# A hybrid attention, state-space and ConvFFN block on one core: other order of products and shared sums in Down's last group, an own bank for its right columns, and two up pairs with the value half first

## The chip, the cores and the metric

One Trainium2 chip, of which the kernel uses one core. The metric is the device time of one execution in microseconds (us), taken as the median over several runs; the profile is of one further execution. Engines go by short names: PE is TensorE (matmuls into PSUM banks), DVE is VectorE, ACT is ScalarE, POOL is GpSimd, SP is SyncE, which here only starts transfers. A queue (SPq, ACTq) is an engine's own list of transfers to start.

## The reference

One layer: a normed input goes through attention and a state-space model side by side, the merged result through an output projection, then a gated feed-forward part with a causal convolution of width 3, and a last norm. All in float32; 1024 tokens after 16 meta tokens, model width 1024, feed-forward width 2816. The change lies in the last two lines of this cut:

```
def _rmsnorm(x, g):
    xf = x.astype(jnp.float32)
    y = xf * lax.rsqrt(jnp.mean(xf * xf, axis=-1, keepdims=True) + RMS_EPS)
    return (y * g.astype(jnp.float32)).astype(x.dtype)

def _conv_ffn(xn, w_up, conv_w, conv_b, w_down):
    seq_len = xn.shape[1]
    hid = xn @ w_up
    hp = jnp.pad(hid, ((0, 0), (CONV_WIDTH - 1, 0), (0, 0)))
    conv = conv_b + sum(hp[:, j:j + seq_len] * conv_w[j] for j in range(CONV_WIDTH))
    val, gate = jnp.split(conv, 2, axis=-1)
    return (jax.nn.silu(gate) * val) @ w_down
...
        xn = _rmsnorm(h, norm_ffn_g[layer])
        h = h + _conv_ffn(xn, w_ffn_up[layer], ffn_conv_w[layer], ffn_conv_b[layer],
                          w_ffn_down[layer])
    h = _rmsnorm(h, norm_final_g)
    return h[:, N_META:]
```

## The kernel before

**A float32 product as three matmuls.** Every operand is cut into a high part (a cast on ACT to the type fp32r) and a low part (source minus high part, `split_lo`, line 137, on DVE or POOL). A product is then high·high + high·low + low·high. The pair of cuts of one operand is called a form here.

**The up stage.** The feed-forward width is 22 blocks of 128 channels; block c of the value and block c of the gate are a pair. Pairs 0, 1, 2 and 21 are "plain" (`plain_steps`, line 1209): for each half the 1024 tokens are taken in parts of 342, 342 and 340, each part 8 × 3 matmuls into one PSUM bank; ACT then writes the first term of the convolution with its bias (line 1228), DVE adds the other two (line 1230). The gate's output is the tile `og`, of which one buffer exists, the value's is `ov`, of which two exist. When both are there, `glue` takes the silu of `og` on ACT, multiplies it into `ov` on POOL (line 1183), and starts the store to `a_d`. The plain pairs do the gate half first. While pairs 0 to 2 run, DVE also makes token forms (`xn_forms`, lines 1349 and 272 to 279) for the pairs 3 to 20, which are made in another way.

**The Down stage** (from line 1386) multiplies the 1024 × 2816 result by the down weights and adds it to the residual, held in eight tiles `hs0` to `hs7` (128 tokens × 1024). It halves all three dimensions, so that a 2 × 2 product of blocks takes seven products of half size instead of eight. `j` counts 11 slices of the inner dimension, in four groups, (8,9), (7,0,1), (2,3,4), (5,6,10). Each group runs the products p in the order 0, 4, 1, 2, 5, 3, 6 (`ORDER`); a product is four tiles t of 128 tokens, each 3 matmuls for every j of its group, so 9 in the last group, 512 columns wide. Upper tiles are `hs0` to `hs3`, lower ones `hs4` to `hs7`, and l_ and r_ their left and right 512 columns.

- *Banks.* Products 0, 1, 2 and 3 take four fresh banks, from one of two sets (`SETS`: banks named mm, mm, mm, po, or sp, tp, sp, tp). Products 4, 5 and 6 go on in the banks of 0, 1 and 3 (`JOINS`), on top of what is there, after DVE has read it.
- *Results.* After each tile DVE adds the bank to where product p goes (line 1517): `u2[t]` (u20 to u23) for 0 and 2, the right half of the lower tile for 1 and 3, the left half of the upper for 4, of the lower for 5, and the right half of the upper for 6.
- *Shared sums.* What `u2` holds after product 2 goes into three places, on POOL (line 1528): the lower tile's left and right half and the upper tile's right half. In groups before the last, `u2` goes on to the next group and is not yet used, so that these sums exist in the last group only: 12 of 128 × 512.
- *Norm.* When a half tile is final, ACT squares it and sums the squares (`square`, line 1476), DVE adds that to the other half's (`va`, line 1478), POOL takes the power −1/2 (`rs`, line 1483), and `finish` scales: the left half, already multiplied by the weight `gfB` on POOL (lines 1531 and 1534), on ACT (line 1486), the right half times `rs` and `gfB` on DVE (line 1484). A transfer of each half follows, from SP for the right one and from ACT for the left one.
- *Forms.* `prepare` makes the forms of coming products as far ahead as there are slots (`ops`), in the order of the products. The low parts are cut on POOL for products 0, 4 and 5, on DVE for the others.
- *The last product* (6) of the last group takes tile 3 in two parts, 288 and 224 columns, both in tile 3's bank.

**What sets the order.** The program gives the instructions and which data each needs. The build orders each engine's instructions by its own planner of time, so that order is not that of the text; `after(x, y)` puts x behind y. On the chip each engine runs its list in that order, and an instruction that has to wait holds up those behind it.

## Time and profile before

| | us |
|---|---|
| runs of the kernel | 1450.41, 1450.68, 1454.93 |
| median | 1450.68 |
| the profiled execution's own time | 1446.98 |
| its span in the profile | 1445.2 |
| granted TensorE clock, mean over the span | 0.997 of full speed |
| PE busy | 1422.3 |
| DVE, POOL, ACT busy | 1074.9, 760.8, 721.4 |

The span runs from the first to the last thing that the profiler recorded; the execution's own time is 1.78 us longer. Busy shares are means over a whole program of unlike stages. In the rows of a timeline stand the start in us from the span's begin, the length, the engine, the line, the instruction with its tiles (buffer numbers left out, so `hs` is any of eight), the shape, and in brackets how long the engine was idle before it and what ended that. Up pairs 0 to 2 lie at about 765 to 843 us, the last group of Down at about 1376 to 1437 us.

The same stretch by engine, from the view of windows (length, then busy us and count of PE, PE's weight load, DVE, ACT and POOL, the granted clock, the DMA engines' share and GB/s):

```
1384.00:1392.00 8.00, 8.00 (x37) 6.64 (x36) 7.83 (x6) 1.86 (x4) 7.10 (x5) 1.00 0.39 118
1392.00:1408.00 16.00, 16.00 (x73) 13.24 (x72) 14.73 (x23) 7.04 (x16) 7.12 (x6) 1.00 0.00 0
1408.00:1417.00 9.00, 9.00 (x41) 7.33 (x40) 4.21 (x7) 2.17 (x6) 9.00 (x8) 1.00 0.01 2
```

### The profile page before, as it was taken

The page shows a single profiled execution, that of the slowest core. Times are in us where ns is not written, and L with a number is a line of the kernel's source. Part 1 is how long each engine was busy: PE and PEld are TensorE (multiplying, and loading weights), DVE is VectorE, ACT ScalarE, POOL GpSimd, SP SyncE. Part 2 cuts the span into 40 slices and gives each one's busy share as a digit, 9 for nine tenths or more (in the row PEclk, how much of TensorE's full clock was granted, in tenths as well). Part 3 has the DMA queues.
Part 4 walks back from the last instruction along what each step waited for, and adds up shares of the span by engine and source line. Part 5 has one row for each costly group of instructions (what it writes and reads, how often), then busy time and mean ns, then how long its engine had stood idle before and what let it go on. Part 6 is the DMA issues. An engine that isn't in the chain of part 4 may idle for free.

```text
span 1445.2 us, 26585 instructions
## 1 busy us (share of the span) xinstructions
PE 1422.3 (98%) x9646; PEld 1346.2 (93%) x9646; DVE 1074.9 (74%) x2199; ACT 721.4 (50%) x1421; POOL 760.8 (53%) x887
## 2 busy tenths in 40 slices
PE   8999999999999999999999999999999999999996
PEld 8999999988999999999889999999999999888885
DVE  7999798833667675656479977788876776789695
ACT  7647585423646565533646444434444445644333
POOL 1542248632456556425861335555555544887866
PEclk9999999999999999999999999999999999999998
DMA  8675644520147412177954246667743327964343
GB/s 302 172 179 164 163 102 146 166 83 31 47 141 166 114 59 78 31 245 251 247 149 145 76 110 168 178 160 189 190 138 111 97 80 255 328 204 146 104 93 117
DMA packets 92968, 214.06 MB, mean 148 GB/s; under 512 B 15090, under 2 KB 22898, under 8 KB 92452
## 3 DMA queue, kind: packets, MB, share of 16 engines
q1 hardware_dynamic: 73124, 166.32, 34.6%
q0 software_dynamic: 17696, 41.29, 14.9%
q10 hardware_dynamic: 2016, 4.74, 0.9%
q8 instruction: 76, 1.25, 0.4%
q14 instruction: 56, 0.46, 0.1%
HBM read 170.88 MB, written 71.71 MB: 168 GB/s over the span
## 4 chain that ended last, share of the span: by engine, by line
PE 93%; DVE 4%; issue 1%; ACT 1%; DMA 1%; POOL 0%; DVEq 0%; SPq 0%; ACTq 0%
PE mm L172 5%; PE mm L170 5%; PE mm L171 5%; PE sp L232 4%; PE sp L233 4%; PE sp L234 4%; PE tp L232 3%; PE tp L233 3%; PE tp L234 3%; PE mm L234 3%; PE mm L232 3%; PE mm L233 3%; PE tp L860 3%; PE mm L1509 2%; PE mm L1507 2%; PE mm L1508 2%
## 5 line engine op out<-in xcount | busy, mean ns | idle before, releaser
L170 PE MATMUL mm<-xhi,whi 128*128 128x342 f32 (+2 forms) x480 | 156.8, 327 | 1.0 <-DVE q L137 1.0
L172 PE MATMUL mm<-xhi,wlo 128*128 128x342 f32 (+2 forms) x480 | 155.3, 324 | 0.0
L171 PE MATMUL mm<-xlo,whi 128*128 128x342 f32 (+2 forms) x480 | 155.2, 324 | 0.0
L1183 POOL TENSOR_TENSOR ov<-ov,og 128x1024 f32<-128x1024 f32 x21 | 51.0, 2428 | 116.5 <-ACT og L1182 112.6
L137 DVE TENSOR_TENSOR sw<-sf,sw 128x512 fp32r<-128x512 f32 x72 | 72.5, 1007 | 45.9 <-ACT sw L1174 45.9
L1174 ACT CAST sw<-sf 128x512 fp32r<-128x512 f32 x72 | 44.9, 624 | 112.3 <-POOL sf L1318 87.5
L170 PEld LDWEIGHTS mm<-xhi,whi 128*128 128x128 f32 x480 | 90.5, 188 | 2.1 <-PE sp L818 0.8
L172 PEld LDWEIGHTS mm<-xhi,wlo 128*128 128x128 f32 x480 | 90.3, 188 | 0.5 <-issue 0.2
L171 PEld LDWEIGHTS mm<-xlo,whi 128*128 128x128 f32 x480 | 90.4, 188 | 0.2
L867 ACT CAST th<-tp 128x256 fp32r<-128x256 f32 (+3 forms) x120 | 56.1, 471 | 62.1 <-PE tp L860 29.8
L1318 POOL TENSOR_TENSOR sf<-raw,sf 128x512 f32<-128x512 f32 x36 | 63.7, 1769 | 40.0 <-DVE sw L137 39.9
L137 DVE TENSOR_TENSOR tl<-tp,th 128x256 fp32r<-128x256 f32 (+3 forms) x120 | 65.2, 547 | 26.0 <-ACT th L867 24.6
L1318 POOL TENSOR_TENSOR sf<-raw 128x512 f32<-128x512 f32 x36 | 48.2, 1338 | 65.0 <-DMA raw<-in_w_up_dram 39.8
L234 PE MATMUL mm<-xhi,sw 128*128 128x258 f32 (+1 forms) x288 | 81.0, 281 | 0.0
L232 PE MATMUL mm<-xhi,sw 128*128 128x258 f32 (+1 forms) x288 | 80.8, 281 | 0.0
L233 PE MATMUL mm<-xlo,sw 128*128 128x258 f32 (+1 forms) x288 | 80.7, 280 | 0.0
L832 POOL TENSOR_SCALAR pt<-pt,nm 128x144 f32<-128x144 f32 (+4 forms) x72 | 52.2, 738 | 50.9 <-DVE nm L831 49.9
L1370 DVE SCALAR_TENSOR_TENSOR ov<-hv,cwt,ov 128x1024 f32<-128x1024 f32 x36 | 69.5, 1930 | 0.4 <-ACT ov L1368 0.4
L1174 ACT CAST sw<-raw 128x512 fp32r<-128x512 f32 x70 | 43.0, 621 | 46.8 <-PE sp L234 22.8
L830 ACT ACTIVATE pt<-pt,nm 128x144 f32<-128x144 f32 (+4 forms) x72 | 52.9, 735 | 25.9 <-DVE nm L829 25.5
L823 DVE CUSTOM_DVE_ANT_0 pt<-sp,fb 128x328 f32<-128x328 f32 (+8 forms) x112 | 46.5, 430 | 20.6 <-PE sp L818 12.1
L137 DVE TENSOR_TENSOR sw<-raw,sw 128x512 fp32r<-128x512 f32 x70 | 57.8, 828 | 4.4 <-ACT sw L1174 4.4
(716 smaller groups left out, 5708.3 us busy)
## 6 DMA issues: line engine op xcount, KB each, us to landing
raw<-in_w_up_dram SPq DMA_DIRECT2D x44, 512.0 KB, 3.7
t_d<-in_w_dn_dram POOLq DMA_DIRECT2D x44, 256.0 KB, 6.9
wr<-t_d SPq DMA_DIRECT2D x44, 256.0 KB, 3.4
ar<-a_d SPq DMA_DIRECT2D x41, 256.0 KB, 5.3
a_d<-ov SPq DMA_DIRECT2D x18, 512.0 KB, 2.6
wr<-in_w_dn_dram SPq DMA_DIRECT2D x33, 256.0 KB, 3.7
t_d<-in_w_dn_dram SPq DMA_DIRECT2D x22, 256.0 KB, 4.3
t_d<-t_d SPq DMA_DIRECT2D x22, 256.0 KB, 4.5
```

The source lines that it names most:

```text
L137: return eng.tensor_tensor(out_, src, hi.bitcast(F), ALU.subtract)
L170: yield PE.matmul(ps, whi[:, i, :], ahi[:, i], start=(i == 0), stop=False)
L171: yield PE.matmul(ps, whi[:, i, :], alo[:, i], start=False, stop=False)
L172: yield PE.matmul(ps, wlo[:, i, :], ahi[:, i], start=False, stop=(i == k - 1))
L232: PE.matmul(ps, a[0][:, i], bh, start=(i == 0 and not joins), stop=False, skip_group_check=True)
L233: PE.matmul(ps, a[0][:, i], bl, start=False, stop=False, skip_group_check=True)
L234: PE.matmul(ps, a[1][:, i], bh, start=False, stop=(i == kh - 1), skip_group_check=True)
L830: S.activation(pt[:n, :kc], pt[:n, :kc], AF.Exp, bias=nm[:n, 1:2], scale=0.125, accum_out=nm[:n, 2:3])
L867: S.copy(th[:kn, z:tw], tp[:kn, z:tw])
L1174: S.copy(hi, src)
L1318: sums.append(GP.tensor_tensor(f_, a, b, op))
L1370: V.scalar_tensor_tensor(out=o, in0=h_[:, j:SEQ + j], scalar=cwc(j, m), in1=o, op0=ALU.mult, op1=ALU.add)
```

## The change

**Plain pairs.** Pairs 1 and 2 do the value half first, then the gate half. Pairs 0 and 21 stay.

**Down, last group only:**

- The products run as 0, 2, 4, 1, 5, 3, 6, and their forms are prepared as 0, 1, 2, 4, 5, 3, 6. Product 2 now takes the other set of banks (mm, mm, mm, po).
- The shared sums are spread: after the tiles of product 2 the one into the lower tile's left half, after those of product 1 the one into its right half, after those of product 5 the one into the upper tile's right half. Their number is the same.
- Products 3 and 6 both take tile 3 in parts of 288 and 224 columns, in this order, as the last tile. The 224 columns of both have a bank of their own (`held["end"]`).
- The scale of a finished tile is put behind the next tile's add (`scale_last`). Tile 2's right half is scaled at the very end; for tile 3, the square of the last 224 columns is taken on DVE, and the right half is multiplied by `gfB` first and by `rs` then (`finish_end`).

**All groups:** the slots of the forms are a list in which a freed slot goes to the back, instead of a counter.

The diff, cut to what is spoken of:

```diff
@@ -1207,14 +1207,17 @@
         return ha.tile([P, SEQ], F, tag=tag, name=tag, bufs=OUTS[tag])
 
     def plain_steps(c, parts=(QBLK,), ws={}):
-        res = []
+        res = {}
         ws = dict(ws)
-        for part, (m, tag) in ((part, mt) for part in parts for mt in ((NFF + c, "og"), (c, "ov"))):
+        halves = ((NFF + c, "og"), (c, "ov"))
+        if c in (1, 2):
+            halves = halves[::-1]
+        for part, (m, tag) in ((part, mt) for part in parts for mt in halves):
...
             if part is parts[0]:
-                res.append(conv_out(m, tag))
-            w2, o = ws[m], res[int(m == c)]
+                res[tag] = conv_out(m, tag)
+            w2, o = ws[m], res[tag]
...
-        glue(*res, c)
+        glue(res["og"], res["ov"], c)
 
     def plain_pair(c):
         run(plain_steps(c))
...
-        slot = ops[n_op[0] % len(ops)]
-        n_op[0] += 1
+        slot = ops.pop(0)
...
-        held[p] = [b() for b in SETS[(g + (p == 1)) % 2]]
+        held[p] = [b() for b in SETS[(g + (p == 1 or p == 2 and g == len(groups) - 1)) % 2]]
         return held[p]
 
     ss = {}
 
-    def square(c, cols):
+    def square(c, cols, by_dve=False):
         s_ = dn.tile([P, 1], F, tag="ss", name="ss", bufs=4)
-        S.activation(sq[:, :cols.stop - cols.start], hs[c][:, cols], AF.Square, accum_out=s_)
+        if by_dve:
+            x_ = hs[c][:, cols]
+            last_ = V.tensor_tensor_reduce(out=u2[0][:, :cols.stop - cols.start], in0=x_, in1=x_, scale=1.0, scalar=0.0,
+                                           op0=ALU.mult, op1=ALU.add, accum_out=s_)
+        else:
+            last_ = S.activation(sq[:, :cols.stop - cols.start], hs[c][:, cols], AF.Square, accum_out=s_)
         va = dn.tile([P, 1], F, tag="va", name="va", bufs=12)
-        V.scalar_tensor_tensor(out=va, in0=s_, scalar=1.0 / D, in1=ss[c] if c in ss else eps, op0=ALU.mult, op1=ALU.add)
+        va_ = V.scalar_tensor_tensor(out=va, in0=s_, scalar=1.0 / D, in1=ss[c] if c in ss else eps, op0=ALU.mult, op1=ALU.add)
         ss[c] = va
-
-    def finish(c, a, b):
+        return last_, va_
+
+    behind_ = []
+
+    def scale_last(inst):
+
+        while behind_:
+            finish(behind_.pop(), inst)
+
+    def finish_end(c, times):
         rs = dn.tile([P, 1], F, tag="rs", name="rs", bufs=2)
         GP.tensor_tensor(rs, ss[c], nhalf, ALU.pow)
-        V.scalar_tensor_tensor(out=hs[c][:, b], in0=hs[c][:, b], scalar=rs, in1=gfB[:, b], op0=ALU.mult, op1=ALU.mult)
+        a_, b_ = HALF
+        sc_ = V.tensor_scalar(hs[c][:, b_], u2[c][:, a_], rs, None, ALU.mult)
+        after(sc_, times)
+        S.activation(hs[c][:, a_], hs[c][:, a_], AF.Copy, scale=rs)
+        SY.dma_start(out[P * c:P * c + P, b_], hs[c][:, b_])
+        S.dma_start(out[P * c:P * c + P, a_], hs[c][:, a_])
+
+    rs_of = []
+
+    def right_half(c, rs, inst):
+        b = slice(512, D)
+        st_ = V.scalar_tensor_tensor(out=hs[c][:, b], in0=hs[c][:, b], scalar=rs, in1=gfB[:, b], op0=ALU.mult,
+                                     op1=ALU.mult)
+        after(st_, inst)
         SY.dma_start(out[P * c:P * c + P, b], hs[c][:, b])
+        return st_
+
+    def finish(c, inst):
+        a = slice(0, 512)
+        rs = dn.tile([P, 1], F, tag="rs", name="rs", bufs=2)
+        GP.tensor_tensor(rs, ss[c], nhalf, ALU.pow)
+        if c == 2:
+            rs_of.append(rs)
+        else:
+            right_half(c, rs, inst)
         S.activation(hs[c][:, a], hs[c][:, a], AF.Copy, scale=rs)
         S.dma_start(out[P * c:P * c + P, a], hs[c][:, a])
 
@@ -1491,12 +1528,13 @@
         joins = p in JOINS
         whole = (0, 512)
         parts = [(t, whole) for t in range(4)]
-        if last and p == 6:
-
-            parts = [(0, whole), (1, whole), (3, (0, 288)), (2, whole), (3, (288, 224))]
+        if last and p in (3, 6):
+            parts[3:] = [(3, (0, 288)), (3, (288, 224))]
+            if p == 3:
+                held["end"] = m_ps()
         bks = banks(g, p)
         for t, (c0, n) in parts:
-            bk = bks[t]
+            bk = held["end"] if last and p in (3, 6) and c0 else bks[t]
             top, bot = hs[t], hs[4 + t]
             to_, o = {0: (u2[t], 0), 1: (bot, 512), 2: (u2[t], 0), 3: (bot, 512),
                       4: (top, 0), 5: (bot, 0), 6: (top, 512)}[p]
@@ -1517,16 +1555,25 @@
                 first_add.append(V.tensor_tensor(to, to, ps, ALU.subtract if p in MINUS else ALU.add))
             if g == 2 and p == 3:
                 GP.dma_start(bot, h_d[P * (4 + t):P * (4 + t) + P], accum_op=ALU.add)
+            if last and p in (3, 6):
+                scale_last(first_add[-1])
             if last and p == 6:
-                square(t, slice(512 + c0, 512 + c0 + n))
-                if (t, c0) == (3, 0):
-                    continue
+                sq_, va_ = square(t, slice(512 + c0, 512 + c0 + n), by_dve=c0 > 0)
+                if t == 3 and c0:
+                    times = V.tensor_tensor(u2[t], hs[t][:, 512:], gfB[:, r_], ALU.mult)
+                    after(times, va_)
+                    finish_end(3, right_half(2, rs_of.pop(), times))
+                if t < 3:
+                    behind_.append(t)
+                continue
+            if last and n == 288:
+                continue
             if not last:
                 continue
-            if p == 2:
-                for d_, op in ((bot[:, l_], ALU.add), (bot[:, r_], ALU.subtract), (top[:, r_], ALU.subtract)):
-                    GP.tensor_tensor(d_, d_, u2[t], op)
-            elif p == 4:
+            if p in (2, 1, 5):
+                d_, op = {2: (bot[:, l_], ALU.add), 1: (bot[:, r_], ALU.subtract), 5: (top[:, r_], ALU.subtract)}[p]
+                GP.tensor_tensor(d_, d_, u2[t], op)
+            if p == 4:
                 square(t, l_)
                 GP.tensor_tensor(top[:, l_], top[:, l_], gfB[:, l_], ALU.mult)
             elif p == 5:
@@ -1534,20 +1581,18 @@
                 GP.tensor_tensor(bot[:, l_], bot[:, l_], gfB[:, l_], ALU.mult)
             elif p == 3:
                 square(4 + t, r_)
-                finish(4 + t, l_, r_)
-            elif p == 6:
-                finish(t, l_, r_)
+                behind_.append(4 + t)
 
     ORDER = (0, 4, 1, 2, 5, 3, 6)
     items = [(g, p) for g in range(len(groups)) for p in ORDER]
+    turns = items[:-len(ORDER)] + [(len(groups) - 1, p) for p in (0, 2, 4, 1, 5, 3, 6)]
+    items[-len(ORDER):] = [(len(groups) - 1, p) for p in (0, 1, 2, 4, 5, 3, 6)]
     ready = {}
-    room = [len(ops)]
 
     def prepare():
 
-        while len(ready) < (len(items) if first_add else 3) and room[0] >= len(groups[items[len(ready)][0]]):
+        while len(ready) < (len(items) if first_add else 3) and len(ops) >= len(groups[items[len(ready)][0]]):
             g, p = items[len(ready)]
-            room[0] -= len(groups[g])
             if p == 0:
                 for j in groups[g]:
                     if j not in SUMMED:
@@ -1556,7 +1601,6 @@
 
...
-    for g, p in items:
+    for g, p in turns:
         prepare()
...
         product(g, p, ready[g, p], g == 0, g == len(groups) - 1)
-        room[0] += len(groups[g])
+        ops += ready[g, p]
```

**Where the instructions move.** Three places. Names: `u20` to `u23` are u2, `ar` and `wr` the raw operands, `op1` to `op5`, `xhi` and `xlo` the slots that hold forms, `ss` a sum of squares.

DVE in the last group, up to the add of product 1's tile 0 into hs4 (the row L1517 or L1555 with hs4). Before:

```order
L137 TENSOR_TENSOR op3_15183<-ar_16350,op3_15183 128x512
L137 TENSOR_TENSOR op3_15183<-wr_16698,op3_15183 128x512
L1517 TENSOR_TENSOR hs3_15230<-hs3_15230,tp_16565 128x512
L1478 SCALAR_TENSOR_TENSOR va_16666<-ss_16664,eps_15225 128x1
L137 TENSOR_TENSOR xhi_97<-ar_16332,xhi_97 128x512
L137 TENSOR_TENSOR xhi_97<-wr_16749,xhi_97 128x512
L137 TENSOR_TENSOR xhi_97<-ar_16340,xhi_97 128x512
L1517 TENSOR_TENSOR hs4_15235<-hs4_15235,mm_16705 128x512
```

Now:

```order
L137 TENSOR_TENSOR xlo_98<-wr_16760,xlo_98 128x512
L1555 TENSOR_TENSOR hs0_15227<-hs0_15227,sp_16562 128x512
L1555 TENSOR_TENSOR hs1_15228<-hs1_15228,tp_16563 128x512
L1484 SCALAR_TENSOR_TENSOR va_16705<-ss_16703,eps_15225 128x1
L1484 SCALAR_TENSOR_TENSOR va_16720<-ss_16718,eps_15225 128x1
L1555 TENSOR_TENSOR hs2_15229<-hs2_15229,sp_16564 128x512
L137 TENSOR_TENSOR xlo_98<-ar_16348,xlo_98 128x512
L137 TENSOR_TENSOR xlo_98<-wr_16767,xlo_98 128x512
L1555 TENSOR_TENSOR hs3_15230<-hs3_15230,tp_16565 128x512
L1484 SCALAR_TENSOR_TENSOR va_16735<-ss_16733,eps_15225 128x1
L1484 SCALAR_TENSOR_TENSOR va_16750<-ss_16748,eps_15225 128x1
L1555 TENSOR_TENSOR hs4_15235<-hs4_15235,mm_16774 128x512
```

Between product 0's last add (u23 from tp) and this add lie 9 form cuts, 4 adds from PSUM and 3 va before; now 12 form cuts (those of products 3 and 6 all), 8 adds (of products 2 and 4) and 4 va.

POOL, the first shared sums. Before, behind the four products of hs0 to hs3 with gfB:

```order
L1531 TENSOR_TENSOR hs2_15229<-hs2_15229,gfB_15222 128x512
L1531 TENSOR_TENSOR hs3_15230<-hs3_15230,gfB_15222 128x512
L1528 TENSOR_TENSOR hs4_15235<-hs4_15235,u20_15231 128x512 x2
L1528 TENSOR_TENSOR hs0_15227<-hs0_15227,u20_15231 128x512
L1528 TENSOR_TENSOR hs5_15236<-hs5_15236,u21_15232 128x512 x2
L1528 TENSOR_TENSOR hs1_15228<-hs1_15228,u21_15232 128x512
```

Now, right behind POOL's last own form cuts:

```order
L137 TENSOR_TENSOR op0_15180<-ar_16354,op0_15180 128x512
L137 TENSOR_TENSOR op0_15180<-wr_16618,op0_15180 128x512
L1575 TENSOR_TENSOR hs4_15235<-hs4_15235,u20_15231 128x512
L1575 TENSOR_TENSOR hs0_15227<-hs0_15227,u20_15231 128x512
L1575 TENSOR_TENSOR hs5_15236<-hs5_15236,u21_15232 128x512
L1575 TENSOR_TENSOR hs1_15228<-hs1_15228,u21_15232 128x512
```

Eight sums (hs4 to hs7 and hs0 to hs3) now stand ahead of the products with gfB, and four (hs4 to hs7) behind them; before, all twelve stood behind.

DVE at the end of the program. Before:

```order
L1517 TENSOR_TENSOR hs3_15230<-hs3_15230,tp_16889 128x288
L1484 SCALAR_TENSOR_TENSOR hs1_15228<-hs1_15228,rs_17004,gfB_15222 128x512
L1478 SCALAR_TENSOR_TENSOR va_17022<-ss_17020,va_16681 128x1
L1517 TENSOR_TENSOR hs3_15230<-hs3_15230,tp_16889 128x224
L1478 SCALAR_TENSOR_TENSOR va_17036<-ss_17034,va_16666 128x1
L1478 SCALAR_TENSOR_TENSOR va_17056<-ss_17054,va_17022 128x1
L1484 SCALAR_TENSOR_TENSOR hs2_15229<-hs2_15229,rs_17038,gfB_15222 128x512
L1484 SCALAR_TENSOR_TENSOR hs3_15230<-hs3_15230,rs_17058,gfB_15222 128x512
```

Now (the two ISA rows are the square with its sum):

```order
L1555 TENSOR_TENSOR hs3_15230<-hs3_15230,tp_16890 128x288
L1484 SCALAR_TENSOR_TENSOR va_17033<-ss_17031,va_16735 128x1
L1555 TENSOR_TENSOR hs3_15230<-hs3_15230,mm_16886 128x224
L1484 SCALAR_TENSOR_TENSOR va_17051<-ss_17049,va_16750 128x1
L1479 ISA u20_15231,ss_17063<-hs3_15230 128x224
L1479 ISA ss_17063 128x1
L1484 SCALAR_TENSOR_TENSOR va_17065<-ss_17063,va_17051 128x1
L1563 TENSOR_TENSOR u23_15234<-hs3_15230,gfB_15222 128x512
L1509 SCALAR_TENSOR_TENSOR hs2_15229<-hs2_15229,rs_17045,gfB_15222 128x512
L1499 TENSOR_SCALAR hs3_15230<-u23_15234,rs_17070 128x512
```

The 224 columns now come from a bank of their own (mm instead of tp), and the two last scales are preceded by the square and the product with gfB.

3 lines of the change are left out of this document (removed).

## The prediction, before the changed kernel was run

> **What bounds the kernel now.** I read the page first, then PE's waits, then the timeline of each engine around the two edited places. From the page, its head, PE's row and the chain of waits:
>
> ```profile
> span 1445.2 us, 26585 instructions
> PE 1422.3 (98%) x9646; PEld 1346.2 (93%) x9646; DVE 1074.9 (74%) x2199; ACT 721.4 (50%) x1421; POOL 760.8 (53%) x887
> PE 93%; DVE 4%; issue 1%; ACT 1%; DMA 1%; POOL 0%; DVEq 0%; SPq 0%; ACTq 0%
> ```
>
> PE is busy 98% of the span and the change takes no matmul away. So only gaps in PE, and what follows its last matmul, can move. The list of what PE waited for (total, times, longest) names the gaps:
>
> ```profile
> PE mm L351 <- ACT uh L409: 5.2, 1, 5.2
> PE tp L1507 <- DVE hs L1517: 3.6, 1, 3.6
> PE mm L1224 <- DVE og L1230: 1.6, 1, 1.6
> ```
>
> The first is at the start of the kernel and is not touched. The other two, 5.2 us together, are what the two edits can remove.
>
> **Part 1: pairs 1 and 2, value half first.** The timelines of PE, POOL, ACT and DVE (start, length, instruction, in brackets the idle time before it):
>
> ```profile
> 810.08 0.39 PE L1224 MATMUL mm<-xhi,sw 128*128 128x344 f32 x1 [1.65 <-DVE og L1230]
> 799.98 2.64 POOL L1183 TENSOR_TENSOR ov<-ov,og 128x1024 f32<-128x1024 f32 x1 [2.39 <-DVE ov L1230]
> 802.83 1.16 ACT L1228 ACTIVATE og<-mm,cwt 128x342 f32<-128x342 f32 x2
> 806.72 0.56 DVE L1230 SCALAR_TENSOR_TENSOR og<-mm,cwt,og 128x342 f32<-128x342 f32 x1
> 808.89 1.04 DVE L1230 SCALAR_TENSOR_TENSOR og<-mm,cwt,og 128x340 f32<-128x340 f32 x2
> ```
>
> The buffer og exists once. Pair 0's glue on POOL reads it until 802.62, so ACT cannot begin to empty pair 1's first gate bank before 802.83, though PE had filled it earlier. DVE's part follows at 806–810, and PE needs that bank again at 808.43. With the value half first the evictions go to ov, which has two buffers, and wait for no glue. They can start some 3 us earlier. Gate's evictions come one half later, when the glue is long over. I take the whole wait, −1.65. Bounds: that, since no other gap of PE lies there, and 0 if the same wait returns at a later bank (a rival below). The cover is the second ov buffer alone; without it the 1.65 is back.
>
> **Part 2: own bank for the right columns.** PE's and DVE's timelines at the end of the last product:
>
> ```profile
> 1429.68 0.39 PE L1507 MATMUL sp<-xhi 128*128 128x512 f32 x1
> 1431.04 0.29 PE L1507 MATMUL tp<-xhi 128*128 128x288 f32 x1
> 1432.09 0.29 PE L1509 MATMUL tp<-xhi 128*128 128x288 f32 x1
> 1435.94 0.37 PE L1507 MATMUL tp<-xhi 128*128 128x224 f32 x1 [3.56 <-DVE hs L1517]
> 1436.92 0.28 PE L1509 MATMUL tp<-xhi 128*128 128x224 f32 x1
> 1435.43 0.45 DVE L1517 TENSOR_TENSOR hs<-hs,tp 128x288 f32<-128x288 f32 x1
> 1437.24 0.39 DVE L1517 TENSOR_TENSOR hs<-hs,tp 128x224 f32<-128x224 f32 x1 [0.24 <-PE tp L1509]
> ```
>
> The 224 columns share the bank tp with the 288, so PE waits until DVE has read those: 3.56 us. The change gives them a bank that product 3 has begun, so nothing is left to wait for: −3.56. For that, product 3's tile 3 is split too, nine matmuls becoming eighteen. From the fence the pitch of a 288 is (1432.09−1431.04)/8 = .131 and of a 224 (1436.92−1435.94)/8 = .122, the first of them slow, thus some .115; a 512 has (1431.04−1429.68)/6 = .227. So 9 × (.131+.115−.227) = +.17; I take +.15.
>
> **What is late next: DVE's last loop.** With that stall gone DVE must finish one tile per PE tile, 9 × .227 = 2.04 us. The changed queues put the scale of a finished tile between two squares on ACT:
>
> ```profile
> 1433.29 0.15 DVE L1478 SCALAR_TENSOR_TENSOR va<-ss,va 128x1 f32<-128x1 f32 x1
> 1433.52 0.55 POOL L1483 TENSOR_TENSOR rs<-va,nhalf 128x1 f32<-128x1 f32 x1 [1.53 <-DVE va L1478]
> 1434.10 0.72 ACT L1486 ACTIVATE hs<-hs,rs 128x512 f32<-128x512 f32 x1
> 1436.36 0.71 ACT L1486 ACTIVATE hs<-hs,rs 128x512 f32<-128x512 f32 x1
> 1436.97 0.61 ACT L1476 ACTIVATE sq<-hs 128x512 bf16<-128x512 f32 x1
> 1437.71 0.16 DVE L1478 SCALAR_TENSOR_TENSOR va<-ss,va 128x1 f32<-128x1 f32 x1
> ```
>
> Round that loop: va to rs .23, rs to scale .58, scale to the next square .61, square to va .74, together 2.16. Eight tiles at 2.16 instead of 2.04 make DVE late by 8 × .12 = +.96 at most; I take +.8, bounds 0 (the loop slips apart) and +1.5.
>
> **The tail after PE.** Now 1437.20 (the last 224's end) to 1445.2:
>
> ```profile
> 1438.53 1.41 DVE L1484 SCALAR_TENSOR_TENSOR hs<-hs,rs,gfB 128x512 f32<-128x512 f32 x2
> 1428.75 11.56 SPq L1485 DMA_DIRECT2D out_dram<-hs  x8
> DMA to landing us min/median/max: 2.0/2.9/3.5
> ```
>
> DVE's last scale ends at 1439.94, 2.74 after PE. Changed: add .39, va .15, the square on DVE (no row of its kind here; between the 224-add's .39 and the .68 of a 512-add, taken .45), va .15, product with gfB .60, tile 2's scale .67, the last scale .45: 2.86. So +.1. One transfer fewer goes out together at the end: −.3 at most, 0 at least; the two cancel.
>
> **Part 3: third product second, shared sums spread.** Both kernels place 12 sums on POOL. Before, they run in one piece after product 2; the change spreads them and lets eight of them start at about 1392, 14 us earlier, when POOL's own forms are done. Rows of POOL and DVE, and PE's first matmul of product 5:
>
> ```profile
> 1383.46 1.29 POOL L137 TENSOR_TENSOR op<-wr,op 128x512 fp32r<-128x512 f32 x1
> 1387.67 1.73 POOL L137 TENSOR_TENSOR op<-ar,op 128x512 fp32r<-128x512 f32 x1
> 1406.41 15.03 POOL L1528 TENSOR_TENSOR hs<-hs,u 128x512 f32<-128x512 f32 x12 [5.50 <-DVE u L1517]
> 1384.77 1.79 DVE L137 TENSOR_TENSOR op<-ar,op 128x512 fp32r<-128x512 f32 x1
> 1386.48 1.78 DVE L137 TENSOR_TENSOR op<-wr,op 128x512 fp32r<-128x512 f32 x1
> 1401.38 0.68 DVE L1517 TENSOR_TENSOR hs<-hs,mm 128x512 f32<-128x512 f32 x1
> 1404.45 0.68 DVE L137 TENSOR_TENSOR xhi<-wr,xhi 128x512 fp32r<-128x512 f32 x1
> 1405.05 0.68 DVE L1517 TENSOR_TENSOR hs<-hs,po 128x512 f32<-128x512 f32 x1
> 1412.87 0.69 DVE L1517 TENSOR_TENSOR hs<-hs,mm 128x512 f32<-128x512 f32 x1
> 1416.77 0.95 DVE L1478 SCALAR_TENSOR_TENSOR va<-ss,eps 128x1 f32<-128x1 f32 x1 [0.84 <-ACT sq L1476]
> 1408.45 0.39 PE L1507 MATMUL mm<-op 128*128 128x512 f32 x1
> ```
>
> A form cut (L137) takes .68 when POOL is idle (1404.45, the next instruction .60 later) and 1.79 while POOL works, in steps of 1.71 (1386.48−1384.77); POOL's own go from 1.29 to 1.73. The two take turns. An add that reads a PSUM bank does not: .69 at 1412.87, in the middle of POOL's 15.03.
>
> In the block of 12 sums (1406.4–1421.4) DVE had no form left. Spread, the sums meet the forms of products 3 and 6. PE's first matmul of product 5, at 1408.45, joins product 1's bank, so it needs the add of product 1's tile 0 first. Before, that is the add at 1401.38, seven us ahead. Changed, product 1 comes fourth, and the order has in front of that add, from 1384.8 on: 12 form cuts, 8 adds from PSUM, 4 va. The first four cuts meet POOL's own forms as before; POOL then has 8 sums of 1.25 (15.03/12), which in turns with the cuts last to about 1406. So 10 cuts at 1.70 and two at .60 are 18.2; 8 adds at .60, 4.8; the va with their waits for ACT about 1.7; the add itself .68: 25.4, thus 1410.2, and PE starts after some .1: **+1.9**. Bounds: 0 (each cut that runs alone saves 1.1, so two of the ten are enough: 1408.0), and +4.3 (12 cuts at 1.79, and one va more that waits as at 1416.77, .84+.95).
>
> [...]
>
> **Before that**, in the joint of the last two groups, DVE has five cuts more than before ahead of one add:
>
> ```profile
> 1366.61 1.87 DVE L1517 TENSOR_TENSOR hs<-hs,mm 128x512 f32<-128x512 f32 x3
> 1367.72 0.39 PE L1507 MATMUL mm<-xlo 128*128 128x512 f32 x1
> ```
>
> The first of these three adds ended about 1367.2, half a us ahead of PE. Five cuts more are 3.0 (.60 each), but POOL's own forms there come later, which returns the turns of the four cuts before the add, 4 × 1.1 = 4.4. I take +.2; bounds 0 and +2.5 (only a fifth of that returned).
>
> **Sum.** −1.65 −3.56 +.15 +.8 +.1 −.1 +1.9 +.2 = −2.2 us. It is made in an execution of 1446.98 us, whose span is 1445.2 and 1.8 lies around it; the median of the runs shown is 1450.68, 3.7 higher. I take the same −2.2 from the median: **1448.5 us**. A change of 0.3%, 4.35 us, is about what a measurement of this kernel can tell from none: faster means below 1446.33, slower above 1455.03.
>
> **Rivals.**
> - No new stall at product 5. For it: the add had 7 us in hand before, and POOL's eight sums last only 10 us if nothing meets them. Against it: 1384.8–1391.6, where each cut took 1.79. Then −2.2−1.9−.2 = −4.3, and −5.1 if the loop does not lag either: 1445.6 to 1446.4.
> - Turns without an end, slower than before. If every cut costs 1.79 (21.5), and each of the four va waits on ACT and POOL as at 1416.77 (4 × 1.79 = 7.2), the add ends at 1384.8+21.5+4.8+7.2+.7 = 1419.0, a stall of 10.6, so +6.5: 1457.2. It decides from a stall of 4.1 on, that is an add that ends after 1412.5. Against it: va's waits there come from squares queued right behind their adds, and in the new order other adds stand between; with half of the va waits the stall is 7 and the time 1453.6.
> - The pairs' gain comes back elsewhere: gate of pair 2 is now the last half before the block pairs and its evictions delay their first bank. DVE has no free moment there, which speaks for it; the banks passed with one wait in the whole stage, which speaks against. Then −.5: 1450.2.
> - The right columns' bank changes nothing, since the end hangs on DVE's add of the 224 columns and not on PE. DVE was idle .24 before it at 1437.24 and reached the 288 only at 1435.43, delayed by va and scales: if DVE stays that late, of the 3.56 only about 1.8 (from 1437.24 back to 1435.43) is won, and the sum is −.5: 1450.2.
>
> **Chances.** The forecast .46, no stall at product 5 .28, turns without an end .10, the pairs' gain returned .06, the end held by DVE .10. Below 1446.33: most of the second case (.24) and the lower edge of the first (.08), together .32. Above 1455.03: over half of the third and a little of the rest, .08. Within: .60. The likeliest case alone spans 1446.5 to 1450.7; the 8 in 10 take in the second case whole and the smaller half of the third: 1445.2 to 1452.5.
>
> **What the changed profile would show.** PE's waits: the row at the 224 columns gone, the row at og gone or under .3, and a new row of some 1.9 us at product 5's first matmul, released by DVE's add of hs4. DVE's cuts between 1392 and 1406 at 1.7–1.8, with POOL's sums at 1.7 instead of 1.25. Steps of 2.1–2.2 between the last squares. I am wrong if PE has no wait at product 5 (then faster), if va is slow beside POOL in a row (then slower), or if a wait appears ahead of 1384.

## The result and the profile after

| | us |
|---|---|
| kernel before, median of 13 runs | 1449.76 (1446.71 to 1457.23) |
| changed kernel, median of 13 runs | 1446.99 (1443.17 to 1449.66) |
| ratio, with its 95% interval | 0.9974 (0.9963 to 0.9985) |
| the changed kernel's profiled execution, its span | 1445.58, 1443.8 |

Faster by 0.26% of the time, 3.8 us by the ratio, 2.8 by the medians. Two later timings beside other kernels gave 0.9969 (0.9958 to 0.9980) and 0.9977 (0.9968 to 0.9986).

The head of the changed kernel's page, and from its list of what PE waited for (total, times, longest) the two entries that stand in Down:

```profile
span 1443.8 us, 26609 instructions
PE 1422.4 (99%) x9655; PEld 1346.2 (93%) x9655; DVE 1074.5 (74%) x2203; ACT 722.4 (50%) x1419; POOL 766.9 (53%) x887
```

```profile
PE mm L1545 <- DVE hs L1555: 1.9, 1, 1.9
PE sp L1545 <- DVE hs L1555: 1.8, 1, 1.8
```

Both waits that the change aimed at are gone, at og (1.65) and at the 224 columns (3.56). Two new ones stand there. The 1.9 is the one forecast at product 5. The 1.8 was not forecast; it lies in the second group of Down, far ahead of the edited code.

The stretch that leads to the 1.9, from the timelines of DVE, POOL and PE:

```profile
1385.14 4.63 DVE L137 TENSOR_TENSOR op<-ar,op 128x512 fp32r<-128x512 f32 x1
1399.12 1.77 DVE L137 TENSOR_TENSOR xlo<-ar,xlo 128x512 fp32r<-128x512 f32 x1
1400.82 1.77 DVE L137 TENSOR_TENSOR xlo<-wr,xlo 128x512 fp32r<-128x512 f32 x1
1406.73 1.77 DVE L137 TENSOR_TENSOR xlo<-wr,xlo 128x512 fp32r<-128x512 f32 x1
1410.03 1.89 DVE L1555 TENSOR_TENSOR hs<-hs,mm 128x512 f32<-128x512 f32 x3
1392.25 12.75 POOL L1575 TENSOR_TENSOR hs<-hs,u 128x512 f32<-128x512 f32 x8 [3.04 <-DVE u L1555]
1410.86 0.47 PE L1545 MATMUL mm<-op 128*128 128x512 f32 x1 [1.89 <-DVE hs L1555]
```

POOL's eight sums last 12.75 instead of the 10.0 that they need alone (8 × 1.25, an estimate from the 15.03 of the twelve sums in the kernel before), DVE's cuts beside them 1.77, and the first of the three adds into hs4, hs5 and hs6 starts at 1410.03, after PE has come to it.

The end of the program, from DVE's and PE's timelines; before, DVE reached the last 224 columns at 1437.24 and ended at 1439.94:

```profile
1431.92 0.16 DVE L1484 SCALAR_TENSOR_TENSOR va<-ss,va 128x1 f32<-128x1 f32 x1 [0.62 <-ACT sq L1482]
1434.11 0.16 DVE L1484 SCALAR_TENSOR_TENSOR va<-ss,va 128x1 f32<-128x1 f32 x1 [0.62 <-ACT sq L1482]
1436.38 0.38 DVE L1555 TENSOR_TENSOR hs<-hs,mm 128x224 f32<-128x224 f32 x1
1438.71 0.48 DVE L1499 TENSOR_SCALAR hs<-u,rs 128x512 f32<-128x512 f32 x1
1435.78 0.28 PE L1547 MATMUL mm<-xlo 128*128 128x224 f32 x1
```

PE ends at 1436.06 and DVE is on the last columns 0.32 later. The steps of the last loop are 2.19 (1434.11−1431.92; 2.16 was worked out).

**A table by stretch.** Single profiles of these kernels differ by up to 7 us before any edited code runs. So every profile below is cut at three points: the first up matmul, Down's first matmul, and the end of DVE's last scale. For the kernel before, and for the changed kernel's third profile (e7), the two first points are PE's rows:

```profile
764.92 0.36 PE L1224 MATMUL mm<-xhi,sw 128*128 128x258 f32 x1
1222.83 0.40 PE L1507 MATMUL mm<-op 128*128 128x512 f32 x1
```

```profile
771.18 0.36 PE L1227 MATMUL mm<-xhi,sw 128*128 128x258 f32 x1
1226.54 0.40 PE L1545 MATMUL mm<-op 128*128 128x512 f32 x1
```

| kernel (profile) | start to up | up to Down | Down to DVE's last scale | from there to the end | lies in the third column |
|---|---|---|---|---|---|
| before | 764.9 | 457.9 | 217.1 | 5.3 | |
| before again, e8 | 767.5 | 457.9 | 218.5 | 4.7 | low clock at the 224 columns |
| changed, first | 765.8 | 455.4 | 218.1 | 4.6 | 1.77 wait in group 2 |
| changed, e1 | 766.5 | 455.4 | 217.5 | 4.6 | low clock in product 5, 1.5 |
| changed, e7 | 771.2 | 455.4 | 216.0 | 4.6 | |
| changed, e11 | 771.5 | 455.4 | 215.9 | 4.6 | |
| pairs only, e6 | 768.3 | 455.4 | 217.3 | 5.3 | 1.0 wait ahead of the last group |
| bank only, e2 | 766.2 | 457.9 | 217.1 | 4.0 | |
| order back, e3 | 765.6 | 455.4 | 216.9 | 5.0 | |
| order without bank, e9 | 764.7 | 456.2 | 217.8 | 4.3 | low clock in product 5, 1.6 |
| cuts on DVE, e5 | 766.6 | 455.4 | 216.6 | 4.6 | 1.74 wait in group 2 |
| cuts on DVE, e10 | 766.4 | 456.0 | 214.5 | 4.6 | |
| order and cuts, e12 | 766.0 | 455.4 | 214.8 | 4.3 | |

The 456.2 of e9 and the 456.0 of e10 come from a wait at 969 that is spoken of under e6.

Without the disturbances, the changed kernel stands at −2.5 (pairs), −1.1 (Down up to DVE's last result) and −0.7 (from there): −4.3 us against the first profile of before. With all disturbances left in, the last three stretches together take 676.9 us in the mean of the changed kernel's four profiles and 680.7 in the mean of the two of before: −3.8, which agrees with the three ratios (−3.3 to −4.5 us).

### The profile page after: what moved, and what is told of

Read it like the earlier page. It is cut to its first block, busy times and chain, and to the rows that moved or that the text cites. A ratio compares the mean times of both kernels' runs of the same rounds, so it can differ in the third digit from the quotient of the medians.

```text
span 1443.8 us, 26609 instructions
## 1 busy us (share of the span) xinstructions
PE 1422.4 (99%) x9655; PEld 1346.2 (93%) x9655; DVE 1074.5 (74%) x2203; ACT 722.4 (50%) x1419; POOL 766.9 (53%) x887
## 3 DMA queue, kind: packets, MB, share of 16 engines
q8 instruction: 76, 1.25, 0.4%
```

## The experiments

**e1, the changed kernel again.** No edit.

> The changed kernel once more, unaltered, for a second profile. In its first profile PE waits 1.89 us at product 5's first matmul (as forecast, 1.9) and, not forecast, 1.77 us in the second group at 1310.6, where one form cut on DVE took 5.96 us while POOL did three cuts in a row. Theory A (who wins between DVE and POOL is chance, and the order of the change has nothing to do with it): the wait in the second group is gone or of another size, the one at product 5 is there again, 1 to 3 us, since it rests on the sum of twelve cuts; the span is about 1442. Theory B (the wait in the second group belongs to the change): 1.7 to 1.8 us at the same place again, span 1443.8 within 0.5.

PE's wait at product 5 is 1.89 again, the one in the second group is gone: theory A on that point. The span is not 1442 but 1444.1, and the cause was in neither theory. The view of windows (us, busy us and count of PE, PE's weight load, DVE, ACT and POOL, then the granted clock) of e1:

```profile
1409.00:1413.00 4.00, 3.42 (x8) 2.70 (x9) 2.22 (x4) 0.00 (x0) 4.00 (x4) 0.59 0.00 0
1413.00:1417.00 4.00, 4.00 (x19) 3.25 (x18) 1.53 (x3) 1.32 (x4) 3.23 (x3) 0.99 0.00 0
```

and its PE rows:

```profile
1409.58 0.66 PE L1545 MATMUL mm<-op 128*128 128x512 f32 x1 [1.89 <-DVE hs L1555]
...
1410.46 0.63 PE L1547 MATMUL mm<-op 128*128 128x512 f32 x1
1410.89 0.63 PE L1545 MATMUL mm<-op 128*128 128x512 f32 x1
```

After the wait the granted clock is 0.59 over four us, and the matmuls follow each other at .43 instead of .23. Product 5 takes 9.9 us up to product 3's first matmul (1409.58 to 1419.52) instead of 8.4 in the first profile (1410.86 to 1419.26): 1.5 us more. The same 1.89 us wait had no such sequel there, nor in e7 (1.92) and e11 (1.88).

**e2, the bank alone, on the kernel before.** With it goes the order of the parts in product 6: tile 2 now comes ahead of both parts of tile 3.

```diff
-        if last and p == 6:
-
-            parts = [(0, whole), (1, whole), (3, (0, 288)), (2, whole), (3, (288, 224))]
+        if last and p in (3, 6):
+            parts[3:] = [(3, (0, 288)), (3, (288, 224))]
+            if p == 3:
+                held["end"] = m_ps()
...
-            bk = bks[t]
+            bk = held["end"] if last and p in (3, 6) and c0 else bks[t]
...
```

> Before, with one thing of the change: products 3 and 6 of the last group take tile 3 in 288 and 224 columns, the 224 in a bank of their own. Products, shared sums, scales and pairs as before. Both theories: PE's wait of 3.56 at the 224 columns is gone. Theory A (the prediction's sum: the end hangs on PE): the end comes 3.4 us earlier, span about 1441.8, ratio to before 0.9977. Theory B (DVE is late at the end, since in before it adds tile 2's columns at 1434.77, 3.7 us after PE had them): the last add can come only behind that one, at about 1435.9 instead of 1437.24, so the end comes 1.0 to 1.5 us earlier, ratio 0.999, and DVE's last adds lag PE by 2 us or more.

Ratio 0.9983 (0.9974 to 0.9992). PE's wait is gone and PE ends early; DVE does not (PE's and DVE's timelines):

```profile
1434.51 0.28 PE L1510 MATMUL mm<-xhi 128*128 128x224 f32 x1
```

```profile
1421.76 0.95 DVE L1478 SCALAR_TENSOR_TENSOR va<-ss,eps 128x1 f32<-128x1 f32 x1 [0.84 <-ACT sq L1476]
1438.23 0.38 DVE L1518 TENSOR_TENSOR hs<-hs,mm 128x224 f32<-128x224 f32 x1
1440.45 0.75 DVE L1484 SCALAR_TENSOR_TENSOR hs<-hs,rs,gfB 128x512 f32<-128x512 f32 x1 [0.66 <-POOL rs L1483]
```

DVE comes to the last columns 3.4 us after PE's last matmul (1434.79). From Down's first matmul to DVE's last scale it is 217.1, to a tenth as without the bank: theory B, and more so than it said. The 1.3 us that the end gained lie behind the last scale (4.0 instead of 5.3). The ratio's −2.5 us is more than that 1.3; that timed runs of before also pay a low clock after the 3.56 us wait, as e8 did, would fit, and was not measured in them; the mean granted clock of those runs, 0.996 or 0.997 in most against 0.997 or 0.998 in those of e2, points the same way.

**e3, products and sums back in the old order, the rest as changed.**

```diff
-        held[p] = [b() for b in SETS[(g + (p == 1 or p == 2 and g == len(groups) - 1)) % 2]]
+        held[p] = [b() for b in SETS[(g + (p == 1)) % 2]]
...
-            if p in (2, 1, 5):
-                d_, op = {2: (bot[:, l_], ALU.add), 1: (bot[:, r_], ALU.subtract), 5: (top[:, r_], ALU.subtract)}[p]
-                GP.tensor_tensor(d_, d_, u2[t], op)
+            if p == 2:
+                for d_, op in ((bot[:, l_], ALU.add), (bot[:, r_], ALU.subtract), (top[:, r_], ALU.subtract)):
+                    GP.tensor_tensor(d_, d_, u2[t], op)
...
-    turns = items[:-len(ORDER)] + [(len(groups) - 1, p) for p in (0, 2, 4, 1, 5, 3, 6)]
-    items[-len(ORDER):] = [(len(groups) - 1, p) for p in (0, 1, 2, 4, 5, 3, 6)]
+    turns = items[:-len(ORDER)] + [(len(groups) - 1, p) for p in ORDER]
+    items[-len(ORDER):] = [(len(groups) - 1, p) for p in ORDER]
```

> The changed kernel with its third part undone: products 0, 4, 1, 2, 5, 3, 6 and all twelve shared sums after product 2, as before; pairs, own bank and scales as changed. Both theories: PE's wait at product 5 is gone. Theory A (the spreading costs 1.9 us and gives nothing else): 1.9 us faster than the changed kernel, ratio to before about 0.9965. Theory B (the spreading also takes POOL's block of sums out of the way of va and rs, so that DVE keeps up with PE at the end): DVE lags PE by 2 to 3.5 us in the last product instead of 0.6, the end is within 1 us of the changed kernel's or later, ratio to before 0.998 to 0.999.

Ratio 0.9978 (0.9968 to 0.9988): the changed kernel's time. Its PE has no wait in Down at all and ends 210.7 us after Down's first matmul (1220.95 to 1431.67), 2.2 ahead of the changed kernel's third profile (212.9), for nothing:

```profile
1431.39 0.28 PE L1547 MATMUL mm<-xhi 128*128 128x224 f32 x1
```

```profile
1421.05 1.05 DVE L1484 SCALAR_TENSOR_TENSOR va<-ss,va 128x1 f32<-128x1 f32 x1 [0.85 <-ACT sq L1482]
1423.55 1.06 DVE L1484 SCALAR_TENSOR_TENSOR va<-ss,va 128x1 f32<-128x1 f32 x1 [0.85 <-ACT sq L1482]
1435.08 0.38 DVE L1555 TENSOR_TENSOR hs<-hs,mm 128x224 f32<-128x224 f32 x1
```

DVE is 3.4 us late. In these rows a va takes 1.05 instead of .16, with .85 of waiting ahead of it, so a tile of product 3 takes DVE 2.5 us (1423.55−1421.05) against PE's 2.04; the last loop's 2.2 can't make it up. The kernel before, with the same order, shows what POOL does beside them: va takes .40 to .95 while POOL does the twelve sums (1406.41 to 1421.44), 1.05 at 1422.90 and 1425.40 beside the four products with gfB that follow (1421.40 to 1426.44), and .16 at 1427.90, behind those. Theory B.

**e4, without the four sums behind product 2** (they are left out, so that hs4 to hs7 lack them in their left halves).

> The changed kernel without the four shared sums behind product 2 (into the left halves of hs4 to hs7), so that part of the result is missing; POOL does only four of the first eight sums while DVE cuts the forms of products 3 and 6. Theory A (the wait at product 5 comes from DVE and POOL taking turns): four collisions of 1.1 us each fall away, the add comes 3 to 4.5 us earlier and PE's wait at product 5 is gone (under 0.2). Theory B (it comes from the number of instructions that now stand ahead of the add, and from va waiting for ACT): the wait stays above 1.3 us.

PE has no wait at product 5. Now POOL does four sums between 1390.88 and 1397.27, and where it is idle DVE's cuts are short again:

```profile
1390.88 6.39 POOL L1575 TENSOR_TENSOR hs<-hs,u 128x512 f32<-128x512 f32 x4 [3.04 <-DVE u L1555]
```

```profile
1396.04 1.77 DVE L137 TENSOR_TENSOR xhi<-wr,xhi 128x512 fp32r<-128x512 f32 x1
1397.73 0.68 DVE L137 TENSOR_TENSOR xlo<-ar,xlo 128x512 fp32r<-128x512 f32 x1
1406.77 1.88 DVE L1555 TENSOR_TENSOR hs<-hs,mm 128x512 f32<-128x512 f32 x3
```

The add comes 23.0 us after the first of the twelve cuts (1383.74 to 1406.77) instead of 24.9 (1385.14 to 1410.03). That is 1.9, less than the 3 to 4.5 expected: only two of the cuts, the ninth and the tenth, become free (.68 instead of 1.77), while the others meet the four sums that are left, or POOL's products with gfB, as in the changed kernel. It is just enough for PE, so theory A. The instructions ahead of the add are the same, so theory B falls.

**e5 and e10, product 5's cuts on DVE**, where it waits for PE anyway (in the changed kernel's first profile 1.15 to 1.38 us ahead of each of the adds from 1376.57 to 1384.53).

```diff
-        eng = GP if p in (0, 4, 5) else V
+        eng = V if p == 5 and j in groups[-1] else GP if p in (0, 4, 5) else V
```

> The changed kernel with one edit: the low parts of product 5's operands in the last group (six cuts, which POOL did at 1380.7 to 1388.2 in the changed kernel's first profile) are cut on DVE, which then waits for PE 1.15 to 1.38 us before each of six adds. So POOL is idle when DVE cuts product 3's first four. Theory A (turn-taking between DVE and POOL sets the wait at product 5, and that wait is what is left to win): those four cuts take 2.4 instead of 6.4, the add into hs4 comes 3 to 4 us earlier, PE's wait at product 5 is gone, the end comes 1.9 us earlier; and so does what the granted clock took after the wait in the second profile (1.75 us, eight matmuls at a pitch of .43 instead of .23). Ratio to before 0.9955 to 0.9965, span 1439.5 to 1441. Theory B (DVE's own load at the end decides, not PE): PE's wait is gone, but DVE lags in the last product by 2 us or more and the end stays within 0.7 us of the changed kernel's.

> Product 5's six cuts on DVE once more, beside the changed kernel on one chip. In its first profile the wait at product 5 was 0.41 instead of 1.9, and a wait of 1.74 in the second group stood beside it. Expected: 0.2 to 0.8 at product 5; from Down's first matmul to the end 219.4 without a wait in the second group, 221.1 with one; 1.0 to 1.5 us faster than the changed kernel, ratio to before 0.0007 to 0.001 lower than that one's.

The wait at product 5 is 0.41 and 0.46. Down up to DVE's last scale takes 214.5 in e10 and 214.8 in e5 less its wait in the second group, 1.2 to 1.5 under the changed kernel. Ratios to before: 0.9962 (0.9949 to 0.9975) beside the changed kernel's 0.9969, and 0.9957 (0.9944 to 0.9970) beside its 0.9977. Both times it is the faster of the two, by 0.07% and 0.20% (0.07% to 0.1% was expected of e10); the intervals overlap, but in the second timing four of its five runs lie below the fastest of the changed kernel's twelve (1444.04). So theory A, without its whole effect: the wait at product 5 shrinks but does not go, as POOL's sums still meet the later cuts (1.77 to 1.79 us for five of them in e10, from 1391.74 on). From e10's timelines:

```profile
1376.35 5.12 DVE L137 TENSOR_TENSOR op<-ar,op 128x512 fp32r<-128x512 f32 x1
1388.00 0.68 DVE L137 TENSOR_TENSOR op<-ar,op 128x512 fp32r<-128x512 f32 x1
```

```profile
1408.60 0.47 PE L1545 MATMUL mm<-op 128*128 128x512 f32 x1 [0.46 <-DVE hs L1555]
```

The first cut is shut out for 5.12 us while POOL does its own for product 4 (POOL is busy for all of 1376 to 1380 and for 0.92 us of 1380 to 1382); then nine more take .68 each, in steps of .60.

**e6, the pairs alone, on the kernel before.** Its edit is the diff's first part.

> Before, with the value half first in pairs 1 and 2 alone. Theory A (the whole wait is won): no wait at og, span 1443.5, ratio 0.9988. Theory B (the wait comes back at a later bank): a wait of 0.5 us or more between 800 and 850, ratio 0.9995 or above.

Ratio 0.9984 (0.9973 to 0.9995). No wait between 800 and 850: theory A. ACT begins to empty pair 1's first bank 31.8 us after up's first matmul (768.30 to 800.07; before 37.9, 764.92 to 802.83), now into ov, while POOL's glue of pair 0 has yet to start:

```profile
800.07 0.64 ACT L1231 ACTIVATE ov<-mm,cwt 128x342 f32<-128x342 f32 x1
803.37 2.39 POOL L1183 TENSOR_TENSOR ov<-ov,og 128x1024 f32<-128x1024 f32 x1 [2.38 <-DVE ov L1233]
```

Up to Down's first matmul it takes 455.4 instead of 457.9: 2.5 us, more than the wait of 1.65. A second wait, 160 us later, is gone too; it stood in the list of before as 0.4. In PE's timeline of before, each of the two waits with the matmul ahead of it and the one behind it (the row at 810.08 stands in the prediction):

```profile
808.15 0.28 PE L233 MATMUL sp<-t1l,sw 128*128 128x256 f32 x1
810.31 0.32 PE L1225 MATMUL mm<-xlo,sw 128*128 128x344 f32 x1
```

```profile
968.54 0.28 PE L234 MATMUL tp<-t0h,sw 128*128 128x258 f32 x1
969.22 0.39 PE L232 MATMUL sp<-t2h,sw 128*128 128x258 f32 x1 [0.39 <-DVE hg L238]
969.44 0.28 PE L233 MATMUL sp<-t2l,sw 128*128 128x258 f32 x1
```

From start to start these waits cost more than the bracket says, since a matmul's row is longer than its step to the next (.28 against .12 ahead of both). At 810 it is 1.93 instead of .12, and the first matmul after it takes .23 instead of .16: 1.9 us lost. At 969 it is .68 instead of .12, and .22 instead of .12: .66. Together that is the 2.5. The second wait is not the swap's alone: it is in all three profiles without the swap (before, e8, e2), but also in two of the eleven with it, as .60 in e9 and .39 in e10, and there the stretch takes 456.2 and 456.0.

The span (1446.2) says nothing here, since this execution started up 3.4 us later than the first of before. A 1.0 us wait ahead of the last group came in too; it came off the wait at the 224 columns (2.42 instead of 3.56), and DVE's last scale came 217.3 after Down's first matmul, as without it (217.1). This is one more sign that DVE, and not PE, held the end.

**e7 and e11, the changed kernel timed beside the others.**

> The changed kernel for a third profile, and timed beside the others. Chance theory: PE's wait at product 5 is 1.5 to 2.5 us again; the wait in the second group is there in at most one of the three profiles; the granted clock after the wait at product 5 either stays at 1.00 or drops for 2 to 4 us as in the second profile. Ratio 0.996 to 0.9985.

> The changed kernel for a fourth profile and a second timing. Expected: 1.8 to 2.0 at product 5 once more; ratio 0.9965 to 0.998; a wait in the second group in one of three profiles so far (it was there in one of the first three), so more likely not.

1.92 and 1.88 at product 5, nothing in the second group, no low clock in Down. Both spans are 1447 all the same, as up starts at 771.2 and 771.5. In e7 PE waited 3.53 us for DVE (line 544) at 198; in e11 it waited 1.82 us for a transfer at 143 and 1.93 us for DVE (line 544) at 199. After the first of these the matmuls came at .32 instead of .18 for 3.5 us (granted clock 0.83 over 196 to 206); after the second the clock was 0.50 over 144 to 146 and 0.77 over 146 to 148; after the third it was 1.00 (198 to 202).

**e8, before again.**

> The kernel before for a second profile. If the first profile (1446.98, below nearly all of its runs) was a lucky execution, this one is 2 to 4 us longer, and the excess stands in PE's waits, in a lower granted clock after one of its waits (1.65 at og, 3.56 at the 224 columns), or at the start; if not, span 1445.2 within 0.7 and the same waits.

Span 1448.6: the first profile was a lucky execution. 2.6 of the 3.4 us are lost before up; the rest is a low clock after the 3.56 us wait, with matmuls at .21 instead of .11 (1.4 us more up to DVE's last scale, .5 less behind it):

```profile
1438.50 0.55 PE L1507 MATMUL tp<-xhi 128*128 128x224 f32 x1 [3.56 <-DVE hs L1517]
1438.86 0.41 PE L1508 MATMUL tp<-xhi 128*128 128x224 f32 x1
1439.07 0.41 PE L1509 MATMUL tp<-xhi 128*128 128x224 f32 x1
```

**e9, the new order without the bank** (product 6 alone takes tile 3 in two parts, both in tile 3's bank), and **e12, the same with product 5's cuts on DVE.**

```diff
-        if last and p in (3, 6):
+        if last and p == 6:
             parts[3:] = [(3, (0, 288)), (3, (288, 224))]
-            if p == 3:
-                held["end"] = m_ps()
...
-            bk = held["end"] if last and p in (3, 6) and c0 else bks[t]
+            bk = bks[t]
```

> The changed kernel without the own bank: products and shared sums in the new order, pairs and scales as changed, but product 6 alone takes tile 3 in two parts and both stay in tile 3's bank. Theory B (the spreading is what lets DVE keep up; bank and spreading need each other): PE waits again ahead of the 224 columns, but only for DVE's add of the 288, 1.0 to 1.8 us instead of 3.56, and the last add comes behind PE at once; from Down's first matmul to the end of the span 221 to 222 (222.4 in the kernel before, 220.7 in the changed one's third profile), ratio to before 0.997 to 0.998. Theory A (the bank alone is worth its 3.4 us, the spreading costs 1.9): the wait is 3 us or more, that stretch 224 or more, ratio above 0.999.

> The changed kernel without the own bank and with product 5's six cuts on DVE. Theory C (after the runs so far: bank and spreading are two remedies for one late DVE, and the second makes the first superfluous): as fast as with the bank, from Down's first matmul to the end 219.1 within 0.5 if no wait in the second group and no drop of the clock lies in it, waits of 0.3 to 0.6 at product 5 and 0.4 to 1.5 ahead of the 224 columns, ratio to before 0.995 to 0.9965. Theory B (they need each other once the wait at product 5 is gone): a wait of 1.5 us or more ahead of the 224 columns, 220 or more, ratio above 0.997.

e9: ratio 0.9964 (0.9952 to 0.9976), beside the changed kernel's 0.9977 and below what either theory had. Its PE row and DVE row at the place of the old 3.56:

```profile
1434.70 0.37 PE L1543 MATMUL tp<-xhi 128*128 128x224 f32 x1 [0.55 <-DVE hs L1553]
```

```profile
1434.19 0.45 DVE L1553 TENSOR_TENSOR hs<-hs,tp 128x288 f32<-128x288 f32 x1 [0.42 <-PE tp L1545]
```

DVE now waits for PE ahead of the 288 columns, and PE for that add alone: 0.55, less than either theory said. Down up to DVE's last scale is 217.8, of which 1.6 is the low clock in product 5 (9.97 us instead of 8.40): 216.2, against 216.0 with the bank. So theory B was right that the bank is not worth its 3.4, and wrong that the two need each other: given the order, the bank adds nothing that shows. e12 says it again without the wait at product 5: 219.1 from Down's first matmul to the end, as e10 (219.1) with the bank, ratio 0.9961 (0.9946 to 0.9975). Theory C.

## Why the prediction came out as it did

The forecast was −2.2 us from the median, within 0.3%; measured −3.8 by the ratio (interval −2.2 to −5.4), with sum and place of most terms right, and one term put to the wrong cause. Of the 1.5 us between the forecast time (1448.5) and the measured median (1446.99), 0.9 comes from the base: the median of before was 1450.68 over three runs and is 1449.76 over thirteen.

- **Pairs, −1.65: mis-sized, −2.5.** The mechanism held (the evictions start 6.1 us earlier, some 3 were worked out) and the rival (the wait returns at a later bank) fell. Of the further 0.9, .2 is what the same wait costs beyond its bracket, and .66 is the wait at 969, which I left out because it lies outside the edited code; it came back in two of the eleven profiles with the swap, so only the 1.9 is safely the swap's.
- **Own bank, −3.56 and +.15: the gap was sized right, its worth was not.** The changed kernel's PE takes 1.5 us less from Down's first matmul to its last, without disturbances (212.9 in e7, 214.4 before), and −3.56+.15+1.9 is −1.5. But e2 and e3 show that a PE freed of the gap, with the old order, ends early and waits for nobody, while DVE ends as before. My rival "the end held by DVE" had this, at a chance of .10 and as half the gain; it is all of it, up to the last scale. The row to read was in the prediction: DVE reached the 288 columns at 1435.43, and PE had done them at 1432.4.
- **Shared sums spread, +1.9 at product 5: right in place, cause and size** (1.89, 1.89, 1.92, 1.88). The twelve cuts take 17.8 where 18.2 was worked out, though DVE does not get every second turn: the first cut was shut out 4.63 us and the next three were free (.68 each). e4 shows that the sums are the cause. Missing in the step: what the spreading gives. It takes POOL's run of sums and products away from va and product 3 (va .16 at 1423.12 and 1425.33 in the first profile, 1.05 in e3), so that DVE follows PE. Net of the wait that it costs it is worth 0.9 in the profiles: DVE's last scale comes 216.9 after Down's first matmul without it (e3) and 216.0 with it (e7; 215.9 in e11). I had entered it as a cost alone.
- **Loop lag, +.8: step right, sum off.** 2.19 per tile (2.16 worked out), but not from the first tile on: DVE's second add of product 3 still waits for PE, and PE's split tile takes 2.2 itself. At the end DVE is 0.32 late.
- **Joint of the groups, +.2: nothing.** No wait there in any of the four profiles of the changed kernel.
- **Tail, 0: −0.25 to the end of the span** (8.0 after PE's last result before, 7.7 now, DVE's 0.32 in it). The last scale, put at .45, took 0.48, as the one TENSOR_SCALAR of its shape in before does (line 1593); the share of the one transfer fewer was my estimate, and no run shows it alone.
- **Rivals.** No stall at product 5: no, but the edit of e5 comes near it (0.41 is left), and is worth 1.2 to 1.5 in Down. Turns without an end: no; the four va and their waits cost 2.3 together, not 7.2.

That the sum came out near is partly luck: the bank's −3.56 counted too much, pairs, spreading and tail too little.

**What stays open.** The 1.77 us in the second group is in two of the eleven profiles with the pairs swapped (the first and e5) and in none of the three without. Code and order are alike there in all of them. DVE's cut began .89 us after POOL's in the changed kernel and .90 in before, and went another way:

```profile
1301.09 5.96 DVE L137 TENSOR_TENSOR op<-ar,op 128x512 fp32r<-128x512 f32 x1
1302.70 1.30 POOL L1440 TENSOR_TENSOR ar<-ar 128x512 f32<-128x512 f32 x1
1303.96 1.30 POOL L137 TENSOR_TENSOR op<-ar,op 128x512 fp32r<-128x512 f32 x1
1305.21 1.30 POOL L137 TENSOR_TENSOR op<-wr,op 128x512 fp32r<-128x512 f32 x1
```

```profile
1302.80 0.94 DVE L137 TENSOR_TENSOR op<-ar,op 128x512 fp32r<-128x512 f32 x1
1303.67 1.78 DVE L137 TENSOR_TENSOR op<-wr,op 128x512 fp32r<-128x512 f32 x1
```

What decides whether DVE gets its turn was not tried.

No run has the new order of the scales without the rest. e3, which has it beside the bank, takes 216.9 and 5.0, e2 with the bank and the old scales 217.1 and 4.0, in one profile each; so no gain of theirs is shown. The third part's 0.9 stands in the profiles alone: e3's ratio (0.9978) does not differ from the changed kernel's three (0.9969 to 0.9977).

## What to carry to other kernels

A wait of the bounding engine is worth only what the engine that releases it can make of it: before the 3.56 us were counted, DVE's row next to them had to be read for how late DVE already was, and two remedies for one late engine must not be added up. Work moved from a block of its own to beside an engine that it takes turns with is paid for (here 1.70 for .60 per cut), which can be worked out from a stretch where the two already meet; it can still pay if what it leaves behind was holding up the end. What a wait costs is read from start to start of the matmuls around it, not from the bracket alone (here 1.9 for 1.65). Where executions differ by more than the edit, cut each profile at fixed instructions and compare stretch by stretch.

## What the runs showed of the hardware that was not expected

- A wait of PE under 2 us was followed by a low granted clock in three profiles (e1 after 1.89 and e9 after 1.90 at product 5: 0.59 over 1409 to 1413 and 0.50 over 1410 to 1412, matmuls at .43 instead of .23, 1.5 and 1.6 us lost; e11 after 1.82 at 143: 0.50 over 144 to 146) and not after four others of 1.88 to 1.93 (product 5 in the first profile, e7 and e11; line 544 in e11: matmuls at .23 in e7, the clock 1.00 in the rest). The 3.56 at the 224 columns was followed by one in e8 (matmuls at .21) and not in before (1.00 over 1435.9 to 1437.3). So the length of the wait alone did not decide it, and no run shows what did.
- DVE and POOL do not take turns strictly. A cut on DVE waited through three or more POOL instructions in a row in the places shown above (4.63, 5.12 and 5.96 us), elsewhere through one (1.78, in before in steps of 1.70 with POOL's at 1.70).
